# A pad of 96 bytes in the constants, and the matrix of head means in the buffer of summed squares

## The chip, the cores and the metric

The kernel runs on one core of a Trainium2 chip. The metric is the device time of one execution in microseconds, the median of several runs. A profile of one execution shows what each engine did: TensorE (PE, with its weight loads as PEld), VectorE (DVE), ScalarE (ACT), GpSimd (POOL) and SyncE (SP), which issues most transfers.

## What is computed

One layer of a streaming encoder on 512 tokens of width 1024, in float32:

```python
h = modulate(rmsnorm(x, norm1_g[l]), sh1, sc1)          # sh, sc, g: c_act @ w_ada + b_ada
gate_b, gate_c, xa, xr, gr = jnp.split(h @ w_in[l], [...], axis=-1)
y_a = gate_b * causal_dwconv(gate_c * xa, conv_a_w[l])
xr = causal_dwconv(xr, conv_b_w[l]) + conv_b_b[l]
y_b = rg_lru(xr, w_r[l], b_r[l], w_i[l], b_i[l], lru_lambda[l]) * jax.nn.gelu(gr)
y = jnp.concatenate([head_rmsnorm(y_a, gn_a[l], 8), head_rmsnorm(y_b, gn_b[l], 8)], axis=-1) @ w_out[l]
x = x + g1[:, None, :] * y
h = modulate(rmsnorm(x, norm2_g[l]), sh2, sc2)
x = x + g2[:, None, :] * peer(h, w_q[l], sub_keys[l], expert_u[l], expert_v[l])
return rmsnorm(x, final_g)
```

`peer` finds for each token and each of 8 heads the 16 best of 128 x 128 experts by two sets of 128 keys. For each chosen expert it takes the dot product of the token with a row of `expert_u`, a gelu and a softmax weight, and adds that multiple of a row of `expert_v`.

## The kernel before

Widths lie on the 128 partitions and the 512 tokens along them while the mixer runs (about 20 to 190 us). Every matrix product of the mixer and of the experts is done in three float32r products: a weight block `wraw` (128 x 1024 float32, 4096 bytes a partition) is loaded, ScalarE rounds it into `whi` (line 72), VectorE makes the remainder `wlo` (line 77), and TensorE multiplies `whi` with the high and the low part of the activations and `wlo` with the high part (lines 86 to 88). Each of wraw, whi and wlo has four buffers.

Then come the experts in two stages. In the stage of u chunks (about 270 to 800 us) the 128 blocks of `expert_u` are multiplied with the later 320 tokens, 24 products of 320 columns a block, while VectorE searches the best keys of the tokens and the gates are built: `jh` and `igh` are one-hot matrices, and line 638 multiplies them into a table of gates that goes through `stg` to memory (`Gd`). In the stage of v chunks (about 800 to 1370 us) the blocks of `expert_v` are multiplied with the gated activations `ch` and `cl` (18 products of 512 columns a block, line 1013); gates and activations come back from memory into `gt`, `h2` and `act`. Beside both stages the first tokens are treated row by row: GpSimd gathers single rows of `expert_u` and `expert_v` (4096 bytes a partition) into `rows` and `rows2` (line 746), and VectorE takes the dot products (767) and the weighted sums (783). In these two stages the order on each engine is the one in which the code is written; before them a scheduler sets it.

Two norms over the width begin with squares: ScalarE squares a block of x, VectorE adds it into `sqa` (128 x 512 float32), and TensorE sums `sqa` over the partitions (line 155, `stat`). The norm over each head of 64 channels multiplies the squares with `hmean`, a matrix with 1/64 in its two diagonal blocks of 64 x 64 (lines 312 and 313, in `head_norm`). The first norm uses `sqa` before the mixer, the second one while `w_out` is applied; `head_norm` lies between.

All tiles are taken from pools that fill the memory of a partition one after the other, `const` first, so a tile in `const` shifts every pool behind it. Pools with `side="right"` fill it from the other end and aren't shifted. The start of the main buffers in bytes, as the built programs have them:

| buffer | before | after |
|---|---|---|
| iota (last constant ahead of the pad) | 18048 | 18048 |
| h2 (activations, later gates) | 19872 = 32 past a multiple of 64 | 19968 = a multiple |
| wraw, whi, wlo (first of each) | 56736, 73120, 89504: 32 past | 56832, 73216, 89600: multiples |
| xs, rows (first) | 105888: 32 past | 105984: a multiple |
| rows2, cf, ch, cl, ys, gt | 168352, 148896, 151968, 158112, 164256, 124320: 32 past | 96 higher: multiples |
| hmean | 126368 (512 bytes) | in sqa |
| sqa | 126880: 32 past | 126464: a multiple |
| sq and the mixer's buffers behind it | 32 past, but vpad (184256) on a multiple | 416 lower: multiples, but vpad 32 past |
| jh, igh, sqd, selT | 140160, 146304, 152448, 135040: multiples | 96 higher: 32 past |
| act, stg, wada, idx_s, acts, h2b (right side) | 32 past | the same |

The 96-byte shift also takes wraw, whi, wlo, rows and rows2 from 160 past a multiple of 256 to a multiple of 256.

Of the kernel before, what the change touches and what calls it, by code (L numbers as in the profile page):

```python
# [8 lines left out]
F32 = mybir.dt.float32  # L9
FR = mybir.dt.float32r  # L10
# [3 lines left out]
AF = mybir.ActivationFunctionType  # L14
OP = mybir.AluOpType
AX = mybir.AxisListType

T = 512
# [16 lines left out]
def block_kernel(ctx, tc, xT, small, w_ada1, w_ada, b_ada, w_in, w_r, w_i, w_out, w_q, keys, uT, u, v, final_g, out):  # L35
    nc = tc.nc
    PS = bass.MemoryType.PSUM

    const = ctx.enter_context(tc.tile_pool(name="const", bufs=1))
# [14 lines left out]
    nc.vector.tensor_scalar(ident, ii, 0.0, None, op0=OP.is_equal)  # L54
    iota = const.tile([128, 128], F32, name="iota")
    nc.gpsimd.iota(iota, pattern=[[1, 128]], base=0, channel_multiplier=0, allow_small_or_imprecise_dtypes=True)
    ones = const.tile([128, 1], F32, name="ones")
    nc.vector.memset(ones, 1.0)
    sel2 = const.tile([128, XB], F32, name="sel2")
# [31 lines left out]
    pers2 = pro.enter_context(tc.tile_pool(name="pers2", bufs=1))  # L91
    xs = pers2.tile([128, KB, T], F32, name="xs")
    for k in range(0, KB, 2):
        nc.sync.dma_start(xs[:, k:k + 2, :], xT[k * 128:(k + 2) * 128, :].rearrange("(k p) t -> p k t", p=128))
    keys_sb = pers2.tile([128, 8, 128], F32, name="keys_sb")
    hmean = pers2.tile([128, 128], FR, name="hmean")
    nc.vector.memset(hmean.bitcast(F32), 0.0)
    for s in range(2):
        nc.vector.tensor_scalar(hmean[64 * s:64 * s + 64, 64 * s:64 * s + 64], iota[64 * s:64 * s + 64, 0:64],
                                0.0, 1.0 / 64, op0=OP.mult, op1=OP.add)  # L100

    psA = pro.enter_context(tc.tile_pool(name="psA", bufs=1, space=PS))
    psZ = pro.enter_context(tc.tile_pool(name="psZ", bufs=1, space=PS))
    sq_pool = pro.enter_context(tc.tile_pool(name="sq", bufs=2))
    sqa = pers2.tile([128, T], F32, name="sqa")

    adac = const.tile([128, 48], F32, name="adac")

# [44 lines left out]
    def stat(src, first, last):  # L153
        for t in range(NT):
            nc.tensor.matmul(pst[:, t:t + 1], src[:, t * 128:(t + 1) * 128], ones,
                             start=first and t == 0, stop=last and t == NT - 1, skip_group_check=True)

    def sq_sum(k, split):
        if k == 0:
            nc.scalar.activation(sqa, xs[:, 0, :], AF.Square)  # L160
            return
        sq = sq_pool.tile([128, T], F32, name="sq")
        if k == KB - 1 and split:
            nc.vector.tensor_mul(sq, xs[:, k, :], xs[:, k, :])
        else:
            nc.scalar.activation(sq, xs[:, k, :], AF.Square)
        if k < KB - 1 or not split:
            nc.vector.tensor_add(sqa, sqa, sq)
        if k == KB - 1:
            stat(sqa, True, not split)  # L170
            if split:
                stat(sq, False, True)
# [6 lines left out]
    for k in range(KB):  # L179
        sq_sum(k, False)  # L180
# [82 lines left out]
    ybuf_l = mixp.tile([128, KB, T], FR, name="ybuf_l")  # L263
    bdh = mixp.tile([128, KB, 128], FR, name="bdh")
    bdl = mixp.tile([128, KB, 128], FR, name="bdl")

    def ada_rest():
        bdr = wring.tile([128, KB, 128], F32, name="wraw", bufs=WR)
        nc.vector.memset(bdr, 0.0)
        for s in range(2):  # L270
            for w, wsrc in enumerate((w_r, w_i)):
                nc.sync.dma_start(bdr[64 * s:64 * s + 64, 4 * w:4 * w + 4, 64 * s:64 * s + 64],
                                  wsrc[s::2].rearrange("h i j -> i h j"))
        nc.scalar.activation(bdh, bdr, AF.Copy)
        nc.vector.tensor_sub(bdl, bdr, bdh.bitcast(F32))
        yield
        yield from ada_group(1)
        grow = yield from ada_group(2)
        for b in range(2):
            nc.sync.dma_start(g2d[b:b + 1, :], grow[32 * (2 + b):32 * (2 + b) + 1, :])  # L280
        nc.sync.dma_start(keys_sb, keys)
        yield
# [47 lines left out]
    for cb in range(4):  # L330
# [24 lines left out]
        s = mt("s")  # L355
# [43 lines left out]
    for m in range(KB):  # L399
        if m + 2 < KB:  # L400
            oraw[m + 2] = load_w(w_out[m + 2])
        hi, lo = split_w(oraw[m])
        ps = psZ.tile([128, T], F32, name="ps_z", bufs=3)
        mm3(ps, hi, lo, lambda k: ybuf_h[:, k, :], lambda k: ybuf_l[:, k, :], kord, True, True)
        nc.vector.scalar_tensor_tensor(xs[:, m, :], ps, adac[:, 16 + m:17 + m], xs[:, m, :], op0=OP.mult, op1=OP.add)
        sq_sum(m, True)
# [760 lines left out]
```

## Time and profile before

| | us |
|---|---|
| median of 3 runs | 1413.57 (1412.25 to 1414.08) |
| the profiled execution | 1412.09 |
| its span, first to last instruction | 1410.3 |
| TensorE busy | 1348.1 |
| VectorE busy | 1244.3 |
| ScalarE busy | 756.5 |
| GpSimd busy | 528.1 |

A row of instruction groups reads: line, engine, operation, output and inputs with their shapes, count | busy us, mean ns of one | idle us of the engine just before them, and what ended most of it. A row of the timeline reads: start and duration in us, engine, line, operation, count, and in brackets the idle time before it with what ended it. A row of stretches gives each engine's busy us and count, the granted clock, the DMA engines' mean busy share (over 1 where packets overlap) and GB/s. A row of waits gives who waited for what: us in total, times, the longest.

### The profile page before, as it was taken

How to read it: one execution, taken by the hardware profiler on the slowest of the kernel's cores; microseconds unless marked ns; L12 is line 12 of the kernel's file. 1: busy time of each engine (PE TensorE's matmuls, PEld its weight loads, DVE VectorE, ACT ScalarE, POOL GpSimd, SP SyncE). 2: the span in 40 equal slices, each digit the busy share in tenths (PEclk: the TensorE clock that was granted, in tenths of full speed). 3: DMA queues.
4: the chain of work that ended last, by engine and by line, in shares of the span. 5: the costliest groups of instructions: out<-in, count | busy, mean ns of one | idle time of the engine just before them, and what ended most of it. 6: DMA issues, size and time to landing. Idle time of an engine off the chain costs nothing.

```text
span 1410.3 us, 21690 instructions
## 1 busy us (share of the span) xinstructions
PE 1348.1 (96%) x7571; PEld 1167.9 (83%) x7571; DVE 1244.3 (88%) x2452; ACT 756.5 (54%) x1237; POOL 528.1 (37%) x334
## 2 busy tenths in 40 slices
PE   5999998999999999999999989999989999999995
PEld 2566786789999999999999978777878787878784
DVE  7687756999999999899999868798989889898998
ACT  3576644435598799856994433323333434343432
POOL 0000000000244334324432426576656565575660
PEclk9999998999999999999999999999999999999998
DMA  8676332234789899889998999999999999999994
GB/s 345 241 282 214 121 90 76 75 108 146 257 323 392 286 371 377 337 270 342 357 377 308 372 376 353 393 363 402 398 402 398 400 397 400 398 401 395 391 372 176
DMA packets 146929, 440.07 MB, mean 312 GB/s; under 512 B 14722, under 2 KB 42370, under 8 KB 144772
## 3 DMA queue, kind: packets, MB, share of 16 engines
q1 hardware_dynamic: 99812, 267.75, 52.2%
q0 software_dynamic: 46720, 169.89, 31.9%
q8 instruction: 59, 0.97, 0.3%
q10 hardware_dynamic: 288, 1.05, 0.2%
q14 instruction: 50, 0.41, 0.1%
HBM read 393.54 MB, written 45.09 MB: 311 GB/s over the span
## 4 chain that ended last, share of the span: by engine, by line
DVE 26%; issue 26%; PE 20%; DMA 18%; POOL 7%; ACT 3%; DVEq 0%; POOLq 0%; SPq 0%; ACTq 0%
DMA wraw<-in_v_dram 12%; POOL rows L746 7%; PE acc L1013 6%; DVE wlo L77 5%; PE ps_z L88 3%; DMA rows<-in_u_dram,idx_b 3%; PE ps_z L87 3%; PE ps_z L86 3%; DVE scr L767 3%; DVE ys L783 3%; DVE cf L899 2%; DMA rows<-in_u_dram,idx_s 2%; DVE cl L910 2%; DVE rep L472 1%; DVE ti L470 1%
## 5 line engine op out<-in xcount | busy, mean ns | idle before, releaser
L72 ACT ACTIVATE whi<-wraw 128x1024 fp32r<-128x1024 f32 x292 | 308.4, 1057 | 375.8 <-DMA wraw<-in_v_dram 197.6
L77 DVE TENSOR_TENSOR wlo<-wraw,whi 128x1024 fp32r<-128x1024 f32 x292 | 355.8, 1220 | 83.2 <-ACT whi L72 78.2
L86 PE MATMUL ps_act<-h,whi 128*128 128x320 f32 x1024 | 322.4, 315 | 1.6 <-ACT sc L511 1.2
L87 PE MATMUL ps_act<-h,whi 128*128 128x320 f32 x1024 | 317.0, 310 | 0.0
L88 PE MATMUL ps_act<-h,wlo 128*128 128x320 f32 x1024 | 316.8, 309 | 0.0
L746 POOL DMA_INDIRECT rows<-in_u_dram,idx_s x128 | 201.7, 1576 | 229.8 <-DVE scr L767 191.4
L746 POOL DMA_INDIRECT rows<-in_v_dram,idx_s x128 | 223.4, 1745 | 131.8 <-DVE ys L783 103.8
L1013 PE MATMUL acc<-whi,ch 128*128 128x512 f32 x750 | 234.3, 394 | 13.8 <-ACT ch L903 8.0
L1013 PE MATMUL acc<-whi,cl 128*128 128x512 f32 x750 | 234.5, 394 | 7.9 <-DVE cl L910 7.9
L1013 PE MATMUL acc<-wlo,ch 128*128 128x512 f32 x750 | 232.4, 391 | 0.0
L86 PEld LDWEIGHTS ps_act<-h,whi 128*128 128x128 f32 x1024 | 193.1, 189 | 2.2 <-ACT sc L511 1.4
L87 PEld LDWEIGHTS ps_act<-h,whi 128*128 128x128 f32 x1024 | 193.0, 189 | 0.2
L88 PEld LDWEIGHTS ps_act<-h,wlo 128*128 128x128 f32 x1024 | 192.7, 188 | 0.0
L1013 PEld LDWEIGHTS acc<-whi,ch 128*128 128x128 f32 x750 | 141.2, 189 | 46.8 <-ACT ch L903 11.5
L746 POOL DMA_INDIRECT rows<-in_u_dram,idx_b x64 | 97.9, 1529 | 212.9 <-DVE scr L767 107.0
L1013 PEld LDWEIGHTS acc<-whi,cl 128*128 128x128 f32 x750 | 140.9, 189 | 41.6 <-DVE cl L910 12.9
L1013 PEld LDWEIGHTS acc<-wlo,ch 128*128 128x128 f32 x750 | 141.8, 189 | 29.9
L783 DVE SCALAR_TENSOR_TENSOR ys<-rows,acts,ys 128x1024 f32<-128x1024 f32 x127 | 162.7, 1281 | 1.6
L767 DVE SCALAR_TENSOR_TENSOR scr<-rows,h2n 128x1024 f16<-128x1024 f32 x128 | 156.3, 1221 | 8.7 <-DMA rows<-in_u_dram,idx_s 7.2
L834 ACT ACTIVATE act<-ps_act 128x320 f32<-128x320 f32 x128 | 55.5, 433 | 103.8 <-PE ps_act L88 100.0
L423 POOL DMA_DIRECT2D x1d<-xn x8 | 4.6, 572 | 269.8 <-ACT xn L422 269.8
L638 PE MATMUL ps_gt<-igh,jh 128*128 128x128 f32 x768 | 97.3, 275 | 2.3 <-ACT igh L630 0.8
(269 smaller groups left out, 1901.9 us busy)
## 6 DMA issues: line engine op xcount, KB each, us to landing
wraw<-in_uT_dram SPq DMA_DIRECT2D x128, 512.0 KB
wraw<-in_v_dram SPq DMA_DIRECT2D x128, 512.0 KB
Gd<-stg SPq DMA_DIRECT2D x46, 512.0 KB
wada<-in_w_ada_dram SPq DMA_DIRECT2D x16, 1024.0 KB
Ad<-act SPq DMA_DIRECT2D x48, 320.0 KB
act<-Ad SPq DMA_DIRECT2D x48, 320.0 KB
h<-Gd SPq DMA_DIRECT2D x12, 1024.0 KB
wraw<-in_w_in_dram SPq DMA_DIRECT2D x20, 512.0 KB
```

The costliest lines, as they stand in the source:

```text
L72: nc.scalar.activation(hi, raw, AF.Copy)
L77: nc.vector.tensor_sub(lo, raw, hi.bitcast(F32))
L86: nc.tensor.matmul(ps, hi[:, k, :], xh(k), start=first and k == ks[0], stop=False)
L87: nc.tensor.matmul(ps, hi[:, k, :], xl(k), start=False, stop=False)
L88: nc.tensor.matmul(ps, lo[:, k, :], xh(k), start=False, stop=last and k == ks[-1])
L638: nc.tensor.matmul(pg[:, :, k], jh[:, k, :], ig[:, k, :], start=True, stop=True)
L746: nc.gpsimd.indirect_dma_start(out=r[:, :], out_offset=None, in_=table, in_offset=bass.IndirectOffsetOnAxis(ap=idxs[:, k:k + 1], axis=0))
L767: nc.vector.scalar_tensor_tensor(scr, rows.pop(n), 1.0, hn, op0=OP.mult, op1=OP.mult, accum_out=dst[:, k:k + 1])
L783: nc.vector.scalar_tensor_tensor(ys, rows.pop(k), acts[:, k:k + 1], ys, op0=OP.mult, op1=OP.add)
L834: nc.scalar.activation(act[c // 2][:, c % 2], ps, AF.Gelu)
L899: nc.vector.tensor_mul(cf[:, :, XB:].rearrange("p c (g t) -> p c g t", t=16), act.pop(vorder[2 * q] // 2).rearrange("p c (g t) -> p c g t" ...
L1013: nc.tensor.matmul(accs[b][e], st[:, bs], mv[:, e * 512:(e + 1) * 512], start=first, stop=last)
```

## The change

Three things are done. A tile of 24 floats that nothing uses (`pad`, 96 bytes) stands behind `iota`. The tile `hmean` is no longer a buffer of its own: it takes the buffer of `sqa`, which the first norm has used by then, and which the second norm takes back; so it is filled where the mixer's buffers are made, no longer at the start. `sqa` is therefore taken where each norm begins.

```diff
     nc.gpsimd.iota(iota, pattern=[[1, 128]], base=0, channel_multiplier=0, allow_small_or_imprecise_dtypes=True)
+    const.tile([128, 24], F32, name="pad")
     ones = const.tile([128, 1], F32, name="ones")
...
     keys_sb = pers2.tile([128, 8, 128], F32, name="keys_sb")
-    hmean = pers2.tile([128, 128], FR, name="hmean")
-    nc.vector.memset(hmean.bitcast(F32), 0.0)
-    for s in range(2):
-        nc.vector.tensor_scalar(hmean[64 * s:64 * s + 64, 64 * s:64 * s + 64], iota[64 * s:64 * s + 64, 0:64],
-                                0.0, 1.0 / 64, op0=OP.mult, op1=OP.add)
...
-    sqa = pers2.tile([128, T], F32, name="sqa")
...
+    sqs = []
+
     def sq_sum(k, split):
         if k == 0:
-            nc.scalar.activation(sqa, xs[:, 0, :], AF.Square)
+            sqs[:] = [pers2.tile([128, T], F32, name="sqa")]
+            nc.scalar.activation(sqs[0], xs[:, 0, :], AF.Square)
             return
+        sqa = sqs[0]
...
     bdl = mixp.tile([128, KB, 128], FR, name="bdl")
+    hmean = pers2.tile([128, 128], FR, name="sqa")
+    nc.vector.memset(hmean.bitcast(F32), 0.0)
+    for s in range(2):
+        nc.vector.tensor_scalar(hmean[64 * s:64 * s + 64, 64 * s:64 * s + 64], iota[64 * s:64 * s + 64, 0:64],
+                                0.0, 1.0 / 64, op0=OP.mult, op1=OP.add)
```

On VectorE the three instructions that fill the head means change their place; on every other engine the order is the same as before. The first place is the additions of squares of the first norm, where before the two fills of the diagonal blocks stood (`l_339` is a small table for the recurrence, `sel_76` a selection matrix):

```order
L168 TENSOR_TENSOR sqa<-sqa,sq 128x512
L54 TENSOR_SCALAR ident<-ii 128x128
L99 TENSOR_SCALAR hmean<-iota 64x64 x2
L60 TENSOR_TENSOR sel_76<-ident 128x64
L168 TENSOR_TENSOR sqa<-sqa,sq 128x512
L253 TENSOR_TENSOR l_339<-l_339 128x4
L168 TENSOR_TENSOR sqa<-sqa,sq 128x512
```

The same place of the changed kernel (its lines are a little shifted, and the table is `l_336`):

```order
L167 TENSOR_TENSOR sqa<-sqa,sq 128x512
L54 TENSOR_SCALAR ident<-ii 128x128
L252 TENSOR_TENSOR l_336<-l_336 128x4
L61 TENSOR_TENSOR sel_77<-ident 128x64
L167 TENSOR_TENSOR sqa<-sqa,sq 128x512
L253 TENSOR_SCALAR l_336<-l_336 128x4
L167 TENSOR_TENSOR sqa<-sqa,sq 128x512
```

The two fills are gone from between the additions, and steps of the small table have moved up. The second place is on VectorE behind the column sums of the first norm, between their scaling (`rs_m`) and the reciprocal of the root (`rstd`), before:

```order
L112 TENSOR_SCALAR rs_m<-ps_col 128x4
L253 TENSOR_TENSOR l_339<-l_339 128x4
L254 TENSOR_SCALAR l_339<-l_339 128x4
L253 TENSOR_TENSOR l_339<-l_339 128x4
L254 TENSOR_SCALAR l_339<-l_339 128x4
L255 TENSOR_TENSOR l_339<-l_339 128x4
L257 TENSOR_SCALAR l_339<-l_339 128x4
L258 SCALAR_TENSOR_TENSOR sp<-l_339 128x4
L114 RECIPROCAL rstd_135<-rs_t 128x4
```

And after (the head means are written as `sqa`):

```order
L107 TENSOR_SCALAR rs_m<-ps_col 128x4
L252 TENSOR_TENSOR l_336<-l_336 128x4
L266 MEMSET sqa 128x128
L253 TENSOR_SCALAR l_336<-l_336 128x4
L268 TENSOR_SCALAR sqa<-iota 64x64
L254 TENSOR_TENSOR l_336<-l_336 128x4
L268 TENSOR_SCALAR sqa<-iota 64x64
L256 TENSOR_SCALAR l_336<-l_336 128x4
L257 SCALAR_TENSOR_TENSOR sp<-l_336 128x4
L109 RECIPROCAL rstd_132<-rs_t 128x4
```

Eight instructions stand ahead of the reciprocal where seven stood: five of the small table and of sp, the memset and the two fills.

## Prediction

> **What bounds the kernel now.** First the page's busy times and slices, to see which engine is never free.
>
> ```profile
> span 1410.3 us, 21690 instructions
> PE 1348.1 (96%) x7571; PEld 1167.9 (83%) x7571; DVE 1244.3 (88%) x2452; ACT 756.5 (54%) x1237; POOL 528.1 (37%) x334
> ...
> DMA  8676332234789899889998999999999999999994
> GB/s 345 241 282 214 121 90 76 75 108 146 257 323 392 286 371 377 337 270 342 357 377 308 372 376 353 393 363 402 398 402 398 400 397 400 398 401 395 391 372 176
> ```
>
> TensorE is busy nearly everywhere, and in the last third the DMA engines are full too, at a flat 400 GB/s. The average hides two different stages, so the next view is a table of stretches: the mixer (20 to 270), the stage of u chunks (270 to 800), the stage of v chunks (900 to 1350), and 50 us inside the last one.
>
> ```profile
> core 0: us, PE busy (x) PEld busy (x) DVE busy (x) ACT busy (x) POOL busy (x), PEclk, DMA share, GB/s
> 20.00:270.00 250.00, 241.39 (x1224) 170.69 (x1217) 186.31 (x370) 139.36 (x193) 4.03 (x7) 0.97 0.50 173
> 270.00:800.00 530.00, 524.74 (x3728) 518.10 (x3727) 509.00 (x1413) 385.73 (x732) 171.70 (x112) 1.00 0.84 301
> 900.00:1350.00 450.00, 434.06 (x1879) 352.84 (x1878) 402.02 (x426) 165.68 (x212) 282.48 (x165) 0.99 1.03 395
> 1050.00:1100.00 50.00, 50.00 (x223) 41.39 (x222) 42.89 (x42) 18.13 (x25) 28.56 (x17) 1.00 1.04 399
> ```
>
> In the u stage TensorE works 524.74 of 530 us and the DMA share is 0.84: matmuls bound it. In the v stage the DMA share is 1.03, and TensorE loses some time: its best 50 us hold 223 matmuls, so the 1879 of the 450 us would fit into 1879 x 50 / 223 = 421 us. About 29 us are therefore lost there to late data. Who is late is told by the waits of that stretch and by the chain of work that ended last (two views, their rows one after the other):
>
> ```profile
> engine line waited for: us in total, times, longest us
> ACT whi L72 <- DMA wraw<-in_v_dram: 195.3, 71, 8.9
> POOL rows L746 <- DVE ys L783: 98.4, 70, 8.1
> ```
>
> ```profile
> DVE 26%; issue 26%; PE 20%; DMA 18%; POOL 7%; ACT 3%; DVEq 0%; POOLq 0%; SPq 0%; ACTq 0%
> DMA wraw<-in_v_dram 12%; POOL rows L746 7%; PE acc L1013 6%; DVE wlo L77 5%; PE ps_z L88 3%; DMA rows<-in_u_dram,idx_b 3%; PE ps_z L87 3%; PE ps_z L86 3%; DVE scr L767 3%; DVE ys L783 3%; DVE cf L899 2%; DMA rows<-in_u_dram,idx_s 2%; DVE cl L910 2%; DVE rep L472 1%; DVE ti L470 1%
> ```
>
> In the v stage ScalarE waits 195 us for weights of v, and that transfer is the largest single piece of the chain, 12% of the span. So addresses can pay in two ways: through the engines' reading and writing (everywhere), or through the transfers (in the v stage, at most the 29 us).
>
> **The change, part by part: the shift of addresses.** No work is added by the pad. The large buffers on the left of the memory, wraw, whi, wlo, h2, rows, rows2, gt, cf, ch, cl and ys, move from 32 past a multiple of 64 to a multiple. The buffers jh, igh, sqd, selT and vpad go the other way, from a multiple of 64 to 32 past it. That is a gift: the profile of before already holds both kinds, and the same operation on both can be compared.
>
> VectorE first. Of the rows below, jh lies on a multiple of 64 and sqa does not; vpad does (plus 4 bytes a tap) and xpad does not.
>
> ```profile
> L168 DVE TENSOR_TENSOR sqa<-sqa,sq 128x512 f32<-128x512 f32 x13 | 8.9, 687 | 2.5 <-ACT sq L166 2.4
> L622 DVE TENSOR_TENSOR jh<-iota,selT 128x512 f32<-128x512 f32 x80 | 54.8, 685 | 0.2 <-PE ps_gt L638 0.2
> L339 DVE SCALAR_TENSOR_TENSOR xc<-xpad,small_sb,xc 128x512 f32<-128x512 f32 x12 | 9.0, 749 | 0.1
> L388 DVE SCALAR_TENSOR_TENSOR acc<-vpad,small_sb,acc 128x512 f32<-128x512 f32 x8 | 6.0, 748 | 1.1 <-ACT acc L386 1.0
> ```
>
> 685 against 687 ns and 748 against 749 ns: within 2 ns the start does not matter. I take 0 for VectorE, and 0 for ScalarE, which has no such pair but works beside the same memory and is busy only 54%. A stage-by-stage bound of 2 ns on the some 2450 VectorE instructions is 5 us of VectorE time, mostly beside the matmuls.
>
> TensorE next: L638 reads jh and igh (both on a multiple), L416 reads xs (32 past one), both as 128-wide float32 products; the weight loads of whi are 32 past.
>
> ```profile
> L86 PEld LDWEIGHTS ps_act<-h,whi 128*128 128x128 f32 x1024 | 193.1, 189 | 2.2 <-ACT sc L511 1.4 <-ACT act L834 0.7
> L638 PE MATMUL ps_gt<-igh,jh 128*128 128x128 f32 x768 | 97.3, 275 | 2.3 <-ACT igh L630 0.8 <-DVE igh L632 0.7 <-DVE jh L622 0.7
> L638 PEld LDWEIGHTS ps_gt<-igh,jh 128*128 128x128 f32 x768 | 93.2, 191 | 3.4 <-ACT igh L630 2.4 <-PE ps_gt L638 0.6 <-ACT stg L647 0.4
> L416 PE MATMUL ps_z<-ident,xs 128*128 128x128 f32 x32 | 5.7, 297 | 0.0
> ```
>
> ```profile
> start us, us, engine line op out<-in xcount [idle before <-releaser]
> 272.82 0.60 PE L416 MATMUL ps_z<-ident,xs 128*128 128x128 f32 x4
> ...
> 500.03 0.31 PE L88 MATMUL ps_act<-h,wlo 128*128 128x320 f32 x1
> ...
> 502.23 0.31 PE L88 MATMUL ps_act<-h,wlo 128*128 128x320 f32 x1
> 502.37 1.83 PE L638 MATMUL ps_gt<-igh,jh 128*128 128x128 f32 x15
> ```
>
> A weight load takes 189 ns off the multiple and 191 ns on it. Less one product's own time at the end of a run, the 15 products of L638 follow each other at (1.83 - 0.275) / 14 = 0.111 us and the four of L416 at (0.60 - 0.297) / 3 = 0.101 us. Again no difference that favours multiples of 64. The big float32r products (15 steps from 500.03 to 502.23, so 0.147 us each at 320 columns) all read buffers that are 32 past, so for them there is no pair; I take 0 by the nearest rows, and keep the other end for a rival.
>
> Transfers: no large transfer of before begins on a multiple of 64, so here the trace holds no pair at all. What it has is the total:
>
> ```profile
> q1 hardware_dynamic: 99812, 267.75, 52.2%
> q0 software_dynamic: 46720, 169.89, 31.9%
> ```
>
> Neither queue's share says what a row of another start would take. The bounds: nothing; and at most the 29 us that TensorE can take back in the v stage before matmuls bound that stage too. Below nothing there is no reason to go for the rows that gain a multiple, and the act ring and stg stay where they were. Between the ends I take 0, since the engines' rows, the nearest there are, showed 0 for the same shift.
>
> **The moved head means.** Three VectorE instructions leave the start and come back behind the first norm:
>
> ```profile
> 0.88 0.17 DVE L97 MEMSET hmean<- 128x128 f32 x1
> ...
> 9.51 0.39 DVE L99 TENSOR_SCALAR hmean<-iota 64x64 fp32r<-64x64 f32 x2
> ...
> 15.10 0.16 DVE L112 TENSOR_SCALAR rs_m<-ps_col 128x4 f32<-128x4 f32 x1 [0.67 <-PE ps_col L155]
> 15.18 0.15 DVE L253 TENSOR_TENSOR l<-l 128x4 f32<-128x4 f32 x1
> 15.30 0.20 ACT L113 ACTIVATE rs_t<-rs_m 128x4 f32<-128x4 f32 x1 [1.78 <-DVE rs_m L112]
> ...
> 16.38 0.16 DVE L258 SCALAR_TENSOR_TENSOR sp<-l 128x4 f32<-128x4 f32 x1
> 16.45 0.17 DVE L114 RECIPROCAL rstd<-rs_t 128x4 f32<-128x4 f32 x1
> ...
> 17.66 2.08 PE L176 MATMUL ps_rs<-ident,rstd 128*128 128x128 f32 x8
> ```
>
> Before, the memset hides under the load of x and the pair stands among the additions of squares. The pair's leaving saves up to 0.39 us ahead of the column sums, and two small steps of the table l, which now stand there, take back as much at worst. Behind rs_m VectorE is what is waited for: ScalarE's root is done at 15.50, and the reciprocal starts at 16.45 because seven small steps, the first at 15.18 and the last at 16.38, stand ahead of it, 0.18 us each. The order of after puts eight there, five of the small ones with the memset and the pair: 5 x 0.18 + 0.17 + 0.39 = 1.46 us against 7 x 0.18 = 1.26 us, so the reciprocal comes 0.2 us later relative to rs_m. The sum of both places lies between -0.2 and +0.2 us; I take +0.2 us, as the order puts two small steps where the pair was, all of it on the path, since the row sums (17.66) wait for rstd and everything of the mixer for them. The DMA queue is not moved, nor is any row of TensorE, ScalarE or GpSimd.
>
> The shared buffer adds two orders: the memset after the column sums' reading of sqa, which rs_m ahead of it has waited for anyway; and the second norm's first square after the last product with the head means.
>
> ```profile
> 180.58 0.39 PE L313 MATMUL ps_rs<-mt,hmean 128*128 128x512 f32 x1
> ...
> 187.50 0.63 ACT L160 ACTIVATE sqa<-xs 128x512 f32<-128x512 f32 x1
> ```
>
> 6.5 us lie between the product's end and that square: 0. If the cover were gone, the square would delay whi of the second output block behind it on ScalarE.
>
> The sum against the profiled execution, whose time is 1412.09 us (span 1410.3 and 1.8 around it): 0 + 0 + 0.2 = 1412.3 us. That execution is 1.5 us under the median of the runs, 1413.57, so the forecast on the median's footing is 1413.7 us: no change. What a measurement of this kernel can tell is about 0.2%, 2.8 us. The likeliest case's own range is 1411 to 1416.5.
>
> **Rivals.** First, transfers into a multiple of 64 are faster. A row of 4096 bytes that begins 32 past touches 65 blocks of 64 where it need touch 64. If a row's time goes by touched blocks, the v stage, 450 us at a share of 1.03, gets 450 / 65 = 7 us shorter, a little more for the rows of 1024 bytes that h2 and gt take in: 1405 us. The 29 us of TensorE leave room for it. For it: the full DMA share and the 195 us of waits. Against it: the sameness of the engines' rows. If the blocks are of 256 bytes, and the 160 bytes between a block's edge and the start of the row cost as much as the row's own, wraw and rows pay for 4256 bytes and would pay for 4096 after: 3.8% of 450 us, and the time is 1396 us. [...] Chance of either size 0.22.
>
> Second, float32r products gain, though float32 ones do not: by the steps above they take in 320 / 0.147 = 2180 columns a us, those of L638 128 / 0.111 = 1150. One block in 21 of a row of 320 words, 5% of 0.147 us, is 7 ns; over 128 x 24 products of u and 128 x 18 of v that is 38 us, or 1376 us. Against it stands the pair of L638 and L416. Chance 0.04.
>
> Third, slower: jh and igh lose their multiple. One block more on the eight of a 512-byte row would make L638's step of 0.111 us 12% longer, 14 ns on each of its 768 products, in the stage where TensorE works 99% of the time: +10.7 us, 1424 us. It decides from 2.8 us / 768 = 4 ns. The equal steps of L416 speak against it. Chance 0.06.
>
> Fourth, the v stage falls into another rhythm of transfers and waits without a cause in the addresses, by 3 to 5 us either way: 0.05 for each side.
>
> **How the numbers follow.** No change 0.58; transfers 0.22, products 0.04 and a better rhythm 0.05 make faster 0.31; gates 0.06 and a worse rhythm 0.05 make slower 0.11. The time is that of the likeliest, 1413.5 us. From 1400 to 1418 the range takes in the first size of the transfers and the rhythms and leaves out the larger gains and the gates, some 0.17 together.
>
> **What would show it.** Right: in the stretch 900 to 1350 the same 395 GB/s and a count near 1879, the same 195 us of waits for weights of v, and rows L168, L622, L86 and L638 within 3 ns. Wrong for transfers: over 400 GB/s in that stretch and fewer waits of whi. Wrong for products: a u-stage step under 0.147 us. Wrong for the gates: L638's 15 products over 1.9 us. The move shows as the reciprocal of rstd some 0.2 us later behind rs_m, and the row sums between 17.5 and 18.4.

## The result and the profile after

The changed kernel takes 1397.99 us (1396.76 to 1399.50, five runs) against 1412.31 us (1411.51 to 1414.08, five runs): a ratio of 0.9895 [0.9881, 0.9909], 14.3 us faster. The forecast was 1413.5, from 1400 to 1418. The profiled execution's span went from 1410.3 to 1396.2 us. Its page (busy times and slices), to be laid beside the page of before:

```profile
span 1396.2 us, 21690 instructions
PE 1343.5 (96%) x7571; PEld 1167.7 (84%) x7571; DVE 1243.7 (89%) x2452; ACT 757.2 (54%) x1237; POOL 531.2 (38%) x334
...
DMA  8676332234789999979999999999999999999994
GB/s 350 236 279 210 126 100 81 76 93 143 242 312 387 316 352 373 384 217 347 355 372 340 329 388 376 385 372 414 401 414 409 415 411 415 413 415 412 407 364 178
```

The busy time of every engine is the same to within 5 us. What is new is in the last line: the flat 400 GB/s of the last third is now 401 to 415. The table of stretches says the same by stage:

```profile
core 0: us, PE busy (x) PEld busy (x) DVE busy (x) ACT busy (x) POOL busy (x), PEclk, DMA share, GB/s
20.00:270.00 250.00, 240.45 (x1215) 170.65 (x1215) 184.84 (x366) 138.73 (x192) 4.02 (x7) 0.97 0.50 173
270.00:800.00 530.00, 524.22 (x3722) 517.53 (x3721) 508.70 (x1415) 385.71 (x731) 171.43 (x112) 1.00 0.84 300
900.00:1350.00 450.00, 442.89 (x1936) 363.21 (x1935) 415.74 (x439) 170.98 (x217) 296.44 (x171) 1.00 1.03 407
1050.00:1100.00 50.00, 50.00 (x222) 41.38 (x222) 45.93 (x45) 18.30 (x23) 31.11 (x19) 1.00 1.04 410
```

Mixer and u stage stand as they were (173 GB/s both times, 301 and 300). Only from 900 to 1350 does anything move: 407 instead of 395 GB/s, 1936 matmuls instead of 1879, at the same DMA share of 1.03. So the DMA engines are as full as before, and each byte costs them less. At 223 in 50 us, the best rate of before (two other stretches of 50 us reach it here too), 1936 matmuls need 1936 x 50 / 223 = 434 us: TensorE now loses 16 us there instead of 29. The waits of that stretch, and one row of the same view before:

```profile
engine line waited for: us in total, times, longest us
ACT whi L73 <- DMA wraw<-in_v_dram: 146.0, 54, 8.3
ACT whi L73 <- PE acc L1017: 102.9, 47, 3.0
POOL rows L750 <- DVE ys L787: 88.3, 74, 6.1
```

```profile
ACT whi L72 <- PE acc L1013: 49.2, 21, 7.9
```

ScalarE waits 146.0 us for weights of v instead of 195.3, and the wait for TensorE to give back a buffer of whi has doubled from 49.2 to 102.9 us: TensorE is nearly the bound of this stage too. The chain of work that ended last agrees:

```profile
PE 66%; DVE 15%; DMA 8%; issue 6%; ACT 4%; DVEq 0%; SPq 0%; ACTq 0%
PE acc L1017 26%; PE ps_act L87 7%; PE ps_act L88 7%; PE ps_act L89 7%; DMA wraw<-in_v_dram 6%; PE ps_gt L642 4%; PE ps_z L89 4%; PE ps_z L88 4%; PE ps_z L87 4%; DVE wlo L78 3%; DVE scr L771 3%; DMA rows<-in_u_dram,idx_s 1%; DVE igh L636 1%; ACT whi L73 1%; DVE jh L626 1%
```

The weights' transfer fell from 12% to 6%, the products of the v stage rose from 6% to 26%. Where the time went is told by the products of `acc` (count, shortest, median and longest ns, first and last start), before and after:

```profile
L1013 PE MATMUL acc<-whi,ch x750: 387/389/795, 832.0 to 1382.3; 128*128 128x512 f32 x188
```

```profile
L1017 PE MATMUL acc<-whi,ch x750: 387/389/796, 831.6 to 1369.6; 128*128 128x512 f32 x188
```

The v stage lasts 538.0 instead of 550.3 us. Of the 14.1 us of span, 12.3 lie in it, 0.4 ahead of it, and 1.4 behind it (28.0 to 26.6 us after the last of these starts).

Each row of a transfer is one packet of a DMA engine in the trace (the 96 transfers of `act` to and from memory, of 128 rows of 2560 bytes each, left 12288 packets of 2560 bytes, before and after). The trace's packet records from 900 to 1350 us, counted by stream, show how the bytes got cheaper. In both kernels the commonest packet of a size takes the same time: 159 ns for 4096 bytes, 102 for 2560, 46 for 1024. What differs is how many take that time and how many longer:

```
share of packets at (or under) the commonest time / mean ns, 900 to 1350 us
          rows and rows2 (4096)   weights (4096)   act (2560)    gates (1024)
before    0.29 / 166.5            0.34 / 164.4     0.30 / 107.1  0.54 / 48.8
after     0.98 / 162.0            0.99 / 160.7     0.99 / 102.4  1.00 / 46.1
```

Before, some seven in ten packets of the large rows were held up by a few ns; after, hardly any is. The act ring, whose start did not move, gained as much as the others. So a packet's own start alone doesn't decide whether it is slow; that something shared by all streams was full is the author's reading of this table. The engines' own work on these buffers did not get faster: ScalarE's rounding of a block took 1057 ns both times, VectorE's remainder 1220 and 1219, its weighted sum of a row 1281 and 1280. What is shared these records don't say; the experiments had to.

### The profile page after: what moved, and what is told of

Read it like the earlier page. It is cut to its first block, busy times and chain, and to the rows that moved or that the text cites. A ratio compares the mean times of both kernels' runs of the same rounds, so it can differ in the third digit from the quotient of the medians.

```text
span 1396.2 us, 21690 instructions
## 1 busy us (share of the span) xinstructions
PE 1343.5 (96%) x7571; PEld 1167.7 (84%) x7571; DVE 1243.7 (89%) x2452; ACT 757.2 (54%) x1237; POOL 531.2 (38%) x334
## 4 chain that ended last, share of the span: by engine, by line
PE 66%; DVE 15%; DMA 8%; issue 6%; ACT 4%; DVEq 0%; SPq 0%; ACTq 0%
PE acc L1017 26%; PE ps_act L87 7%; PE ps_act L88 7%; PE ps_act L89 7%; DMA wraw<-in_v_dram 6%; PE ps_gt L642 4%; PE ps_z L89 4%; PE ps_z L88 4%; PE ps_z L87 4%; DVE wlo L78 3%; DVE scr L771 3%; DMA rows<-in_u_dram,idx_s 1%; DVE igh L636 1%; ACT whi L73 1%; DVE jh L626 1%
## 5 line engine op out<-in xcount | busy, mean ns | idle before, releaser
L73 ACT ACTIVATE whi<-wraw 128x1024 fp32r<-128x1024 f32 x292 | 308.6, 1057 | 377.6 <-DMA wraw<-in_v_dram 148.4
L78 DVE TENSOR_TENSOR wlo<-wraw,whi 128x1024 fp32r<-128x1024 f32 x292 | 355.6, 1219 | 67.5 <-ACT whi L73 59.5
L771 DVE SCALAR_TENSOR_TENSOR scr<-rows,h2n 128x1024 f16<-128x1024 f32 x128 | 156.2, 1220 | 9.8 <-DMA rows<-in_u_dram,idx_s 8.3
```

Source lines behind the costliest of these rows:

```text
L73: nc.scalar.activation(hi, raw, AF.Copy)
L78: nc.vector.tensor_sub(lo, raw, hi.bitcast(F32))
L771: nc.vector.scalar_tensor_tensor(scr, rows.pop(n), 1.0, hn, op0=OP.mult, op1=OP.mult, accum_out=dst[:, k:k + 1])
```

## The experiments

Three theories stood at the start: transfers want a multiple of 64; they want a multiple of 256; or the move of the head means, not the addresses, made the difference.

### One part alone, and other starts

The head means moved, without the pad:

```diff
-    const.tile([128, 24], F32, name="pad")
```

> The pad alone is left out; the head means still lie in the buffer of summed squares. The buffers of weights, rows and gates start at 416 past a multiple of 512 (32 past one of 64), as in the kernel before. If the addresses make the gain, the time is that of the kernel before, 1410 to 1414 us, and 395 GB/s from 900 to 1350. If the shared buffer or the moved fills make it, 1396 to 1400 us.

Measured: 1413.25 against 1413.89 us, ratio 1.0 [0.9987, 1.0013]. The moved head means and their buffer make nothing of the 14 us that can be told (the interval is 1.8 us either way). From 900 to 1350:

```profile
900.00:1350.00 450.00, 435.39 (x1880) 354.18 (x1879) 402.15 (x428) 165.80 (x211) 282.57 (x166) 0.99 1.03 395
```

A pad of 32 bytes in place of 96, which puts the same buffers on a multiple of 64, but 64 off one of 128 and of 256:

```diff
-    const.tile([128, 24], F32, name="pad")
+    const.tile([128, 8], F32, name="pad")
```

> A pad of 32 bytes in place of 96: the buffers start at 448 past a multiple of 512, so on a multiple of 64, not of 128 or 256. If a multiple of 64 is what counts, 1396 to 1400 us and about 407 GB/s. If it takes a multiple of 256, or if the bytes between a 256-byte edge and the start are paid for, 1408 to 1414 us.

Measured: 1414.04 against 1413.89 us, 1.0006 [0.9993, 1.0019]. Multiples of 64 are not what counts:

```profile
900.00:1350.00 450.00, 431.49 (x1867) 350.90 (x1866) 400.59 (x425) 164.28 (x209) 278.82 (x165) 0.99 1.03 394
```

Two kernels without a pad, in which another constant is made smaller: the first puts the buffers 384 past a multiple of 512 (a multiple of 128 alone), the second 256 past one (a multiple of 256, not of 512).

```diff
-    const.tile([128, 24], F32, name="pad")
...
-        m = const.tile([128, 64], F32, name="rs_m")[:, :n]
+        m = const.tile([128, 56], F32, name="rs_m")[:, :n]     # off384
+        m = const.tile([128, 24], F32, name="rs_m")[:, :n]     # off256
```

> No pad; a constant that is used in 16 of its 256 bytes is made 32 bytes smaller, and the buffers start at 384 past a multiple of 512, so on a multiple of 128, not of 256. By multiples of 64: 1396 to 1400 us. By multiples of 256, or paid bytes ahead of the start (128 of them against 160 before): 1406 to 1413 us.

> The same constant made 160 bytes smaller: the buffers start at 256 past a multiple of 512. By multiples of 64 or of 256: 1396 to 1400 us. If only a multiple of 512 or a whole page counts, 1408 to 1414 us.

Measured: off384 1412.98 us, 0.9994 [0.9982, 1.0007]; off256 1397.54 us, 0.9884 [0.9865, 0.9903], both against 1413.89. The stretches, off384 first:

```profile
900.00:1350.00 450.00, 435.87 (x1876) 356.12 (x1875) 402.29 (x427) 165.45 (x211) 284.87 (x166) 0.98 1.03 395
```

```profile
900.00:1350.00 450.00, 444.70 (x1944) 364.95 (x1944) 416.82 (x442) 170.84 (x218) 299.63 (x172) 1.00 1.03 407
```

The whole gain comes with a multiple of 256 and none of it with one of 128. The counterpart to share_only is the kernel of before, with the head means in their own buffer at their old place, and smaller constants that bring the buffers to a multiple of 512:

```diff
-        m = const.tile([128, 64], F32, name="rs_m")[:, :n]
-        t = const.tile([128, 64], F32, name="rs_t")[:, :n]
+        m = const.tile([128, 16], F32, name="rs_m")[:, :n]
+        t = const.tile([128, 8], F32, name="rs_t")[:, :n]
```

> The other half alone: the head means keep their own buffer and are filled at the start as in the kernel before, and the buffers of weights, rows and gates are brought to multiples of 512 by making two constants smaller. If the addresses are the whole of it: 1396 to 1400 us. If the shared buffer has a part that shows only with the addresses: over 1402 us.

Measured: 1398.33 against 1414.37 us, 0.9896 [0.9879, 0.9912], with 407 GB/s from 900 to 1350. The addresses alone give all of it.

### Which stream must be aligned

First one group of buffers was taken off the multiple while the rest stayed on it: in rows_off rows, rows2, gt, cf, ch, cl and ys (32 past), in weights_off xs, h2, wraw, whi and wlo (160 past).

```diff
+    rowp.tile([128, 8], F32, name="padr")            # rows_off, with the pad of 24 in const
...
-    const.tile([128, 24], F32, name="pad")           # weights_off
+    rowp.tile([128, 24], F32, name="padr")
```

> As the changed kernel, but 32 bytes ahead of rows push rows, rows2, gt, cf, ch, cl and ys to 32 past a multiple of 256; weights stay on a multiple. If each row of a transfer pays for its own start: the rows and gates are some 6 in 10 of the v stage's bytes, so about 1406 us. If one stream off the multiple slows all: 1411 to 1414 us. If only the weights' transfers matter: 1396 to 1400 us.

> The reverse: xs, h2 and weights at 160 past a multiple of 256 as before, rows, rows2, gt, cf, ch, cl and ys on a multiple. If each row pays for itself: the weights are some 4 in 10 of the v stage's bytes, so about 1403 to 1405 us. If one stream off the multiple slows all: 1411 to 1414 us. If only the gathered rows matter: 1396 to 1400 us.

Measured: rows_off 1409.57 us, 0.9966 [0.9952, 0.9981]; weights_off 1408.76, 0.9961 [0.9949, 0.9974], against 1414.37. Each alone seemed to cost over 10 of the 14 us, more than a sum allows. Two rows of rows_off, and the waits of weights_off, show why the reading by streams is spoiled:

```profile
900.00:1350.00 450.00, 446.32 (x1909) 357.85 (x1908) 410.95 (x435) 167.80 (x213) 290.76 (x170) 1.00 1.03 403
1050.00:1100.00 50.00, 50.00 (x216) 40.25 (x215) 44.33 (x43) 18.99 (x24) 30.29 (x19) 1.00 1.04 402
```

```profile
ACT whi L72 <- PE acc L1017: 139.4, 59, 3.2
ACT whi L72 <- DMA wraw<-in_v_dram: 124.6, 44, 7.9
```

TensorE is busier than after (446.32 of 450 us) and yet does fewer matmuls (1909): in 50 us without a gap it does 216 where it did 222 and 223. The step from product to product is 231 to 238 ns in both kernels instead of 227. Both had moved whi against ch, so they changed something on TensorE too. Three kernels on the base of off256 move only what transfers fill, and one moves only what no transfer touches (`ch` and `cl`), all by 32:

```diff
+    rowp.tile([128, 8], F32, name="padr")                          # rows_only: rows
+                rowp.tile([128, 56], F32, name="padr2")            #   back again for what follows
+    gp.tile([128, 8], F32, name="padg")                            #   rows2
...
+    wring.tile([128, 8], F32, name="padw", bufs=1)                 # weights_only: wraw
+            split.append(wring.tile([128, 56], F32, name="padw2", bufs=1))   # whi, wlo stay
...
+                vp.tile([128, 8], F32, name="padc", bufs=1)        # ch_off32: ch, cl
+    gp.tile([128, 56], F32, name="padg")                           #   rows2 stays
```

> All buffers on a multiple of 256 except the gathered rows (rows, rows2), which begin 32 past. ch, cl and the weights are equally placed, so the products keep their step of 227 ns. If each row pays for its own start: the gathered rows are half of the v stage's bytes, so half of the gain is lost, about 1405 us. If one stream off the multiple slows all: 1411 to 1414 us. If the rows do not matter: 1396 to 1400 us.

> All on a multiple of 256 except wraw, the loaded weights, which begin 32 past; whi and wlo, which TensorE reads, stay on it. If each row pays for its own start: a third of the v stage's bytes, 1402 to 1404 us. If one stream slows all: 1411 to 1414 us. If the weights' transfers do not matter: 1396 to 1400 us.

> All transfers on a multiple of 256 as in the fastest kernels; only ch and cl, which no transfer touches and which TensorE takes as weights of the products with v, begin 32 past. If the product's step of 232 to 235 ns in the two kernels before comes from stationary and moving operand being differently placed: that step here too, 407 GB/s or less at a flat 215 to 216 products per 50 us, and 1405 to 1410 us. If it came from the transfers: 227 ns and 1396 to 1400 us.

Measured against 1414.90 us: rows_only 1397.27, 0.9882 [0.9860, 0.9905]; weights_only 1399.32, 0.9887 [0.9858, 0.9916]; ch_off32 1404.87, 0.9945 [0.9927, 0.9964]. The stretch of rows_only, of weights_only, and two of ch_off32:

```profile
900.00:1350.00 450.00, 443.06 (x1938) 363.87 (x1937) 415.94 (x439) 171.05 (x218) 294.74 (x171) 1.00 1.03 407
```

```profile
900.00:1350.00 450.00, 441.66 (x1928) 361.59 (x1927) 413.33 (x438) 169.37 (x217) 293.04 (x170) 1.00 1.02 404
```

```profile
900.00:1350.00 450.00, 448.16 (x1915) 358.89 (x1915) 413.22 (x435) 169.76 (x216) 279.59 (x169) 1.00 1.02 404
1050.00:1100.00 50.00, 50.00 (x216) 40.27 (x215) 45.30 (x44) 18.91 (x24) 32.30 (x19) 1.00 1.04 413
```

Neither stream alone costs anything that can be told from off256 (the four runs of weights_only lie apart, two near 1396 and two near 1402, and the profiled one is the slowest); and ch_off32, where every transfer is aligned, loses 7 us to slower products. If one stream alone costs nothing and all together 14 us, the cost doesn't add up by streams. With rows, rows2 and wraw off together, 32 past, by the same pads and with the smaller constants of align_only:

> Both transfers at once: wraw, rows and rows2 begin 32 past a multiple of 256, everything that TensorE reads and the gates' buffers stay on it. If two limits stand one behind the other (the DMA engines at 159 ns a row whatever its start, the way into the memory at 163 ns a row off the multiple and less on it), then each alone stays under the first limit and both together pass it: 1408 to 1413 us and 396 to 400 GB/s. If the loss of the kernel before came from what TensorE, VectorE or ScalarE read, and not from transfers: 1396 to 1401 us.

Measured: 1401.93 against 1414.89 us, 0.9907 [0.9874, 0.9941]. Both forecasts missed: some 3 to 4 us of the 14 are lost where 10 or more, or none, had been expected. The loss is small against the noise: the interval overlaps those of rows_only and weights_only, though all four runs (1400.47 to 1404.58) lie above every run of off256 (1396.31 to 1398.07).

```profile
900.00:1350.00 450.00, 440.88 (x1920) 361.41 (x1919) 411.39 (x437) 169.13 (x216) 287.77 (x169) 0.99 1.03 403
```

Clearer is the share of packets of weights at 159 ns: 0.97 in weights_only, 0.51 in rows_weights and 0.34 before. That looks like a limit that only many such rows together reach. Of the transfers that moved, the gates alone are on the multiple here and were off it before; a kernel with every transfer off and the operands of TensorE in place was not run, so the other 10 us are not shown by a run of their own. The other way round, act and stg were put on the multiple as well:

```diff
+    sel.tile([128, 56], F32, name="pads")            # on off256
```

> Nearly everything on a multiple of 256: besides the left buffers also act (written out and read back) and stg (written out), by 224 bytes at the other end of the memory. If each row pays for its own start, act is 8% of the v stage's bytes and the gain at most 1 us: 1395 to 1399 us. If one stream off the multiple slows all, act would have held back the changed kernel: 1390 us or less.

Measured: 1398.30 against 1414.90 us, 0.9885 [0.9863, 0.9907], 407 GB/s. Nothing more is to be had from them; of all versions none is faster than the changed kernel by more than the intervals.

### The transfers by themselves

To measure the price without the kernel around it, nothing is computed: 56 blocks of 128 rows of 4096 bytes are loaded, each stage with its buffers 0, 32, 64, 128, 160 and again 0 past a multiple of 256; then blocks are stored (0 and 160 past), then both in turn.

```diff
+    for past in (0, 32, 64, 128, 160, 0):
+        stage(past, True, False)
+    for past in (0, 160):
+        stage(past, False, True)
+    for past in (0, 160):
+        stage(past, True, True)
```

> Nothing is computed (the output is zeros): SyncE alone loads 56 blocks of 128 x 4096 bytes into eight buffers at 0, 32, 64, 128, 160 and again 0 past a multiple of 256, then stores 56 blocks from 0 and from 160 past, then does both in turn. If a row that begins inside a 256-byte piece pays once: the loads at 0 are fastest, the other four some 3% slower and alike. If it pays by the bytes ahead of its start: slower by 0.8, 1.6, 3.1 and 3.9%. If it takes two queues side by side: all alike. The stores show whether reading this memory pays too.

Measured, a stretch inside a stage each: loads 0, 32, 160 past (410 GB/s in the stages of 64 and 128 too), and 0 again; stores 0 and 160 past; both in turn, 0 and 160 past.

```profile
core 0: us, DVE busy (x) POOL busy (x), PEclk, DMA share, GB/s
10.00:70.00 60.00, 0.00 (x0) 0.00 (x0) 1.00 1.03 420
85.00:145.00 60.00, 0.00 (x0) 0.00 (x0) 1.00 1.03 410
...
310.00:370.00 60.00, 0.00 (x0) 0.00 (x0) 1.00 1.03 410
384.00:444.00 60.00, 0.00 (x0) 0.00 (x0) 1.00 1.03 420
465.00:510.00 45.00, 0.00 (x0) 0.00 (x0) 1.00 1.03 420
540.00:585.00 45.00, 0.00 (x0) 0.00 (x0) 1.00 1.02 406
605.00:730.00 125.00, 0.00 (x0) 0.00 (x0) 1.00 1.03 420
750.00:875.00 125.00, 0.00 (x0) 0.00 (x0) 1.00 1.03 420
```

Off the multiple costs 2.4% of a load stream's rate (410 against 420 GB/s), the same at 32, 64, 128 and 160 past; of the stores' rate it takes 3.3% (406 against 420). Loads and stores in turn lose nothing (420 both times), though in the last stage all their rows are off the multiple: there only half of the traffic goes each way, so a limit behind the engines, if that is the cause, would have to count each way by itself. No run shows this directly. It fits the u stage, where gates are stored and table blocks loaded: 0.86 of the 4096-byte packets took the commonest time there before already, and its rate did not change. But at a DMA share of 0.84 that stage was not full, so it proves nothing by itself. Last, loads of which 0, 2, 4, 6, 7 and 8 of every 8 blocks lie 160 past:

```diff
+    for off in ((), (0, 4), (0, 2, 4, 6), (0, 1, 2, 4, 5, 6), (0, 1, 2, 3, 4, 5, 6), range(8)):
+        stage(off)
```

> Nothing is computed (the output is zeros): SyncE alone loads 64 blocks of 128 x 4096 bytes six times, of which 0, 2, 4, 6, 7 and 8 in every 8 begin 160 past a multiple of 256 and the others on it. By two limits in a row: 420 GB/s up to about half, then falling to 410 at all. If every row off the multiple costs its 4 ns: a straight line from 420 to 410, so 415 at half.

```profile
core 0: us, DVE busy (x) POOL busy (x), PEclk, DMA share, GB/s
10.00:80.00 70.00, 0.00 (x0) 0.00 (x0) 1.00 1.03 420
92.00:162.00 70.00, 0.00 (x0) 0.00 (x0) 1.00 1.03 420
176.00:246.00 70.00, 0.00 (x0) 0.00 (x0) 1.00 1.03 420
260.00:330.00 70.00, 0.00 (x0) 0.00 (x0) 1.00 1.03 416
344.00:414.00 70.00, 0.00 (x0) 0.00 (x0) 1.00 1.03 413
428.00:498.00 70.00, 0.00 (x0) 0.00 (x0) 1.00 1.03 410
```

With up to half of the rows off the multiple the rate stayed at 420 GB/s; six, seven and eight of eight cost 4, 7 and 10 GB/s. Two limits in a row would give just this; that is the author's estimate, worked out from these rates. The first would be the 420 GB/s themselves, the most that any of these stages reached (16 x 4096 bytes in some 156 ns). The second would count pieces of 256 bytes: the line 416, 413, 410 goes on to 434 at none off, and 410 x 17 / 16 = 435.6, since a row of 4096 bytes covers 17 such pieces in part or whole when it starts off the multiple and 16 when it starts on it. So placed, the second limit would be hidden behind the first, and with over some 0.6 of the rows off it would come in front. No run reaches 435 GB/s and none shows the pieces: both are estimated from the stages at 410 to 416.

In the kernel this is an estimate from the packets counted between 900 and 1350 us, each row with one piece more where it starts off the multiple, at 256 bytes a piece and 435.6 GB/s. Before: 21160 rows, 13608 weight rows, 5950 of act and 19460 gate rows (1024 bytes, 5 pieces instead of 4) are 693,628 pieces and 60,178 extra, 443 of the 450 us: by this estimate the limit is reached. After: 423 us; weights_only 428, rows_only 436, rows_weights 440. That is the order in which none, none, none and some of the time was lost. That 443 costs 14 us and 440 only 3 to 4 is steeper than this average over 450 us can explain. The same count in slices of 10 us sets them further apart: over 0.99 of the limit lie 34 of the 45 slices before, 19 in rows_weights, 12 in rows_only, 2 in weights_only and none after (0.975 at most). No slice passes 1.02 in any of the five (1.014 at most before), as it must be if the estimate of 435.6 is a limit.

### The products by themselves

TensorE alone, 108 products of 128 x 512 float32r a stage as the v stage has them; the stationary operand `ch` starts 0 to 224 past a multiple of 256 in steps of 32, then both operands 32 past, only the moving one 32 past, `ch` 16 past, and both 0.

```diff
+    for n, (a, c) in enumerate(((0, 0), (8, 0), (16, 0), (24, 0), (32, 0), (40, 0), (48, 0), (56, 0), (8, 8), (0, 8), (4, 0), (0, 0))):
+        stage(n, a, c)
```

> Nothing of the layer is computed (the output is zeros): TensorE alone runs 12 times 108 products of 128x128 by 128x512 float32r in the order of the v chunks; the stationary operand begins 0, 32, 64, 96, 128, 160, 192, 224 bytes past a multiple of 256 and the moving one on it, then both 32 past, then only the moving one, then the stationary 16 past, then both on it. If the difference of the two starts decides: 227 ns at equal starts, 32 past both included, and 231 to 235 at 32 past one. If it is any start off a multiple of 64: 231 to 235 with both 32 past too. If no transfer runs beside, perhaps no difference at all.

Measured: the mean step is 228 ns with both at 0 (the last stage; the first has 14 longer steps at its start) or both 32 past. It is 234 to 235 ns with `ch` 16, 32, 64, 96, 160 or 224 past, 233 at 128 and 230 at 192, and 234 with only the moving operand 32 past. Stretches of 20 us (a matmul that crosses an edge is counted): `ch` 32 past, both 32 past, only the moving operand 32 past, both at 0.

```profile
36.00:56.00 20.00, 20.00 (x87) 16.13 (x86) 0.00 (x0) 0.00 (x0) 0.00 (x0) 1.00 0.00 0
...
216.00:236.00 20.00, 20.00 (x90) 16.53 (x89) 0.00 (x0) 0.00 (x0) 0.00 (x0) 1.00 0.00 0
241.00:261.00 20.00, 20.00 (x87) 16.10 (x86) 0.00 (x0) 0.00 (x0) 0.00 (x0) 1.00 0.00 0
...
293.00:313.00 20.00, 20.00 (x90) 16.57 (x89) 0.00 (x0) 0.00 (x0) 0.00 (x0) 1.00 0.00 1
```

At full clock and with no transfer under way the step is 1 to 3% longer where the two starts differ. This is what spoiled rows_off and weights_off. Before and after do not differ in it: there whi, wlo, ch and cl were all 160 past, or all on the multiple.

## Why the prediction was wrong, point by point

**What bounds the kernel** was read rightly: TensorE in the u stage, transfers in the v stage, and at most 29 us for TensorE to take back. 12.3 us came back in the v stage, and the DMA rate and the waits of whi were the rows that moved.

**VectorE and TensorE at 0** held. The same groups after:

```profile
L167 DVE TENSOR_TENSOR sqa<-sqa,sq 128x512 f32<-128x512 f32 x13 | 8.9, 686 | 2.3 <-ACT sq L165 2.2
...
L626 DVE TENSOR_TENSOR jh<-iota,selT 128x512 f32<-128x512 f32 x80 | 54.7, 683 | 0.1
```

sqa gained its multiple of 64 and went from 687 to 686 ns, jh lost its own and went from 685 to 683. The large products kept their steps of 0.147 and 0.227 us.

**Transfers at 0** is the step that failed: "Between the ends I take 0, since the engines' rows, the nearest there are, showed 0 for the same shift." The term was not 0 but -14 us: from 900 to 1350 the rate rose from 395 to 407 GB/s and the waits for weights of v fell from 195.3 to 146.0 us. The rows were not near by resource: an engine's reading of a partition said nothing of a DMA engine's packets into it. Nor did they reach far enough by address: jh, igh and selT start 128 past a multiple of 256 and vpad 192 past, so no pair held a start on a multiple of 256, the only kind that paid. What the trace did hold was a row of the resource itself. By itself, a DMA share of 1.03 at a flat 400 GB/s doesn't say whether the engines or something behind them is full, but the packet records of the same execution point to it: in the v stage 0.29 of the gathered rows' packets and 0.34 of the weights' took 159 ns or less, and the rest mostly a few ns more (means 166.5 and 164.4). In the u stage, with the same addresses, 0.86 of the 4096-byte packets took 159 ns or less and the few others far longer (mean 183 ns, before and after). Here this small stretch of single packets, in every stream (0.46 to 0.71 of them), was the sign of a possible gain that a mean over queues hides; that a shared limit caused it is inferred, not shown.

**The moved head means** were forecast at +0.2 us, from the reciprocal coming later behind rs_m. The timeline after:

```profile
14.89 0.16 DVE L107 TENSOR_SCALAR rs_m<-ps_col 128x4 f32<-128x4 f32 x1 [0.68 <-PE ps_col L150]
...
16.16 0.17 DVE L109 RECIPROCAL rstd<-rs_t 128x4 f32<-128x4 f32 x1
...
17.44 1.32 PE L175 MATMUL ps_rs<-ident,rstd 128*128 128x128 f32 x8
```

The reciprocal comes 1.27 us behind rs_m instead of 1.35, and the row sums start 0.2 us earlier than before. From the first small step to the reciprocal 1.20 us passed (14.96 to 16.16) where the prediction had added up 1.46: the sum of the steps' own times is too long, as they overlap a little. So the sign of the term was wrong, and it was as small as forecast: nothing that share_only can tell.

**First rival, transfers.** Its second size was right in condition (a multiple of 256) and in time (1396 us): starts on a multiple of 256 gained 16 us (off256, 1397.54 against 1413.89), of 128 or 64 none (off384 1412.98, pad32 1414.04). The price the prediction worked out, of the 160 bytes ahead of the start, no run shows; the runs showed the same loss at 32, 64, 128 and 160 past (410 against 420 GB/s) in its place. By the prediction's own price, 160 of 4256 bytes, a load 32 past would have lost a fifth of what one 160 past loses. So the close time owes something to chance: in place of the 3.8% it took from the v stage the estimate by pieces has 1 in 17 of a limit, bounded by the 420 GB/s that the aligned loads reached on one side and by TensorE on the other. The direction did not decide: loads into a partition paid (410) as stores out of it did (406). The rival's first size, blocks of 64 (1405 us), fell with pad32.

**Second, third and fourth rival.** The products did not gain from a multiple. Gates on jh and igh did not slow: 16 products took 1.95 us, less one's own time (1.95 - 0.275) / 15 = 0.112 us against 0.111. No rhythm was needed. The chance of 0.22 for the transfers was too small for the one resource that was full, had no pair of rows, and gained its multiple of 256 on its two largest streams; the range ended at 1400 because that case was left outside it.

## What to carry to other kernels

Where the profile shows a stage at a full DMA share, look at how long single packets take and not at the mean: here 0.46 to 0.71 of the packets of a size, in every stream, took a little longer than the commonest time (rows of 4096 bytes 166.5 and 164.4 ns in the mean against 159), and putting the rows' starts in a partition on a multiple of 256 bytes (not 64, not 128) brought the v stage from 395 to 407 GB/s; loads of such rows by themselves ran at 420 instead of 410. What was full was not shown. An operand's price may be carried over to another operand only on the same resource; where the trace has no pair for the resource that is full, the range has to reach to the far bound. When such an experiment moves buffers, see that nothing else moves against each other: here float32r products of 512 columns took 228 ns a step where the stationary and the moving operand started equally modulo 256, and 230 to 235 where they didn't.

## What the runs showed of the hardware that was not expected

- Loads of 4096-byte rows into the partitions run at 410 against 420 GB/s when the rows start off a multiple of 256, the same at 32, 64, 128 and 160 past; stores out of them at 160 past run at 406 against 420. With loads and stores in turn nothing is lost (420 both times).
- The loss isn't the sum of its parts: with half of the rows off the rate was still 420 GB/s, with six, seven and eight of eight 416, 413 and 410. In the kernel, rows off alone and weights off alone gave 1397.3 and 1399.3 us, both together 1401.9 (four runs each, with intervals that overlap), everything 1412 to 1414.
- A float32r product of 512 columns takes a step of 228 ns where both operands start at the same place modulo 256, and 230 to 235 ns where they don't, with no transfers about. In the kernel that was 216 instead of 222 products in 50 us, and 7 us of the whole. Why was not found.
